# A hybrid decoder layer on one core: output tiles ahead of the last head's decays, a pin on a second group of side work, and token operands made inside the delta rule

## The chip, the cores and the metric

The kernel runs on one core of a Trainium2 chip. The metric is the device time of one execution in microseconds (us); lower is better. The engines are named as in the profile: PE (TensorE), DVE (VectorE), ACT (ScalarE), POOL (GpSimd) and SP (SyncE, which here only issues transfers). Each engine executes its own instructions strictly in the order in which they stand in its queue.

## What is computed

One layer over 1024 tokens of width 1024, in float32: a SwiGLU feed-forward block of width 2816 (FFN1), a mixer, a second feed-forward block (FFN2), a final norm.

```
x += 0.5 * swiglu(rms_norm(x))                       # FFN1
proj = rms_norm(x) @ w_in                            # q,k,v,z of 8 delta-rule heads; x,z,B,C of the SSM
o_gdn = gated_delta_rule(conv_silu(q), conv_silu(k), conv_silu(v), g, beta)   # 8 heads of 128
o_gdn = rms_norm(o_gdn) * silu(z)
o_ssm = grouped_rms_norm((ssd_scan(xs, dt, a, B, C) + xs * d) * silu(z_ssm))  # 16 heads of 64
x += concat(o_gdn, o_ssm) @ w_out
x += 0.5 * swiglu(rms_norm(x))                       # FFN2
out = rms_norm(x)
```

In the delta rule a head's keys are normalised to unit length, and a chunk's triangular system is solved from the decayed products of the keys with themselves.

## The kernel before

A float32 product is made of three matmuls of rounded parts: each operand is split into `hi` (a cast on ACT) and `lo` (a subtraction on DVE), and `mm3` (L123 to L125) adds hi*hi, lo*hi and hi*lo in one PSUM bank. Sums of quadrants (a seven-product scheme) save matmuls in the feed-forward blocks and in half of the projections; their sums are further DVE work. PSUM has four groups of banks by tag: `pj` with three banks, `mx` with two, `sc` with two, `oo` with one. A list scheduler lays out each engine's queue from the order of the program, the pools' buffers, and pins: inside `with tc.issue_after(ins)` an instruction stands behind `ins` on that one's engine.

FFN1 (`gate_up_all`) runs over steps `i`, in each of which `prep(grp)` makes the next weights' operands for two groups (`as` sums on DVE at L317, `ah` casts on ACT at L241, `al` differences on DVE). It also draws on a generator `side` of weight units for the mixer (`win_units`): a unit is loaded (`wraw`), summed (`wsum`), split (`wunit`) and stored in DRAM (`wu_scr`). In FFN2 the generator is empty. A silu at L380 is the first function of FFN1 on ACT that needs another table (ACT_TABLE_LOAD).

The mixer goes through the SSM in four units `un` of the loop that follows, then through the delta rule's eight heads `h`. The heads 0 to 3 (`NESTED` = 4) are projected by `mm3` through `proj_half`; the heads 4 to 7 by `chunk`, which multiplies the stored weight units (`wunits`) with token operands: sums of token quadrants, made by `token_operands(k)` (11 sums on DVE, four casts `thi`, four subtractions `tlo`, eight stores to `t_scr`) and loaded again by `first_token_tiles`, `token_tile` and others.

A head runs so: `dt` holds its decays (a load, an exponential `qe` at L1361, a causal mask on POOL, eight exponentials at L1364); q, k and v are convolved and put through silu; `k_part` transposes the keys (L1345, eight matmuls into two `mx` banks) and reads each of the eight blocks twice on ACT, `jd` (L1349, a square with its sum) and `kd` (L1350, a scaled copy); the products of the keys (L1426, L1427) use the same two `mx` banks; then come the triangular solve (`fs_u`, `fx`, `ft`, `fs_x`, `lv`), which goes through DRAM, and a chain of eight state steps (L1534 to L1556, with `vn` and `vr` on ACT). The state steps of head h - 1 are interleaved with the projections of head h. `qsq` (L1448) reuses the buffer of `zc`, and so stands behind the store of it to `z_scr`.

In the last head the first output tiles fill PE: `out_start` loads the first SSM group `y` and rows `x` of w_out, splits `x` into `w` and `y` into `mtt` (ACT at L1200, DVE at L1201), and `group_tile(0, b, dh)` for four values of `b` and two of `dh` makes eight tiles of six matmuls in `pj`; ACT scales each into `xa` (L1220), which empties its bank. `group_prep(1)` makes the operands of the next SSM group (`whi`, `wlo` of the weights, `mtt` from `nat`). The remaining groups follow, and then the tiles of the delta rule's heads.

Of the kernel before, what the change touches and what calls it, by code (L numbers as in the profile page):

```python
# [11 lines left out]
F32 = mybir.dt.float32  # L12
F32R = mybir.dt.float32r
# [31 lines left out]
def kernel(  # L45
# [182 lines left out]
    def hsl(h, k, s):  # L228
        return h[k // 2][:, k % 2, s]
# [124 lines left out]
    def gate_up_all(pool, H, w_gate, w_up, scr, raws, ops, last, work, tail, side):  # L354
# [66 lines left out]
        for i, (p, w) in enumerate(todo):  # L421
# [7 lines left out]
            def prep(grp):  # L429

                if nxt:
                    made = a_ops(pool, *((raws[0], m, nxt[0]) for m in A_GROUPS[grp]))
                    if i == 2 and grp == 0:
                        first_hid(made)
                    with ExitStack() as pins:
                        if i == 4 and grp == 0:
                            for e in made:
                                pins.enter_context(tc.issue_after(e.ins))
                        for _ in range(0 if i < 4 else 2 if grp and i % 3 == 1 else 1):
                            next(side, None)  # L440
                elif tail:
                    tail.pop(0)()
                if raws and grp == 1:
                    next_load()
# [541 lines left out]
    def token_operands(k):  # L986

        b11, b12, b21, b22 = ([hsl(t, k + 4 * i, slice(j * 512, (j + 1) * 512)).bitcast(F32) for t in (hhi, hlo)]
                              for i in range(2) for j in range(2))

        def put(m, t):
            hi = tt.tile([P, 512], F32R, name="thi")
            lo = tt.tile([P, 512], F32R, name="tlo")
            split(hi, lo, t)
            for i, part in enumerate((hi, lo)):
                nc.sync.dma_start(out=t_scr[m][:, i, k], in_=part.bitcast(F32))

        def step(t, x, y, op):
            V.tensor_tensor(out=t, in0=x, in1=y, op=op)

        t = tt.tile([P, 512], F32, name="tsum")
        step(t, b22[0], b12[0], ALU.subtract)
        step(t, t, b22[1], ALU.add)
        step(t, t, b12[1], ALU.subtract)
        put(7, t)
        step(t, t, b11[0], ALU.add)
        step(t, t, b11[1], ALU.add)
        put(6, t)
        step(t, b22[0], t, ALU.subtract)
        step(t, t, b22[1], ALU.add)  # L1010
        put(5, t)
        for x, y in ((b21[0], b22[0]), (b21[1], b22[1])):
            step(t, t, y, ALU.subtract)
            step(t, t, x, ALU.add)
        put(4, t)

    tt = cs_.enter_context(tc.tile_pool(name="tokens", bufs=1, side="right", reuse_waits="tile"))
    rstd_g = []
    for un in range(4):
# [36 lines left out]
        token_operands(un)  # L1056
# [154 lines left out]
    def group_tile(n, b, dh, w, m):  # L1211
        bs = slice(b * P, (b + 1) * P)
        ds = slice(dh * 512, (dh + 1) * 512)
        p = psum("pj")
        for j in range(2):
            last = mm3(p, m[0][:, j, bs], m[1][:, j, bs], w[0][:, j, ds], w[1][:, j, ds], j == 0, j == 1)
        o = out_bufs[0][b // 2][:, b % 2, ds]
        r = rstd_g[n // 2][:, b:b + 1]
        if n == 0:
            A.mul(out=o, in_=p, mul=r)  # L1220
        else:
            V.scalar_tensor_tensor(out=o, in0=p, scalar=r, in1=o, op0=ALU.mult, op1=ALU.add)
        return last

    FIRST_TILES = 4
    out_bufs, ready0 = [], []

    def out_start():
# [8 lines left out]
        for j in range(2):  # L1237
            split(w[0][:, j], w[1][:, j], x[:, j])
            ssm_split(0, j, y, *m)
# [87 lines left out]

    slots, H_IN = [], {}
# [3 lines left out]
    first_token_tiles()  # L1332
    with ExitStack() as cg:
        g1 = cg.enter_context(tc.tile_pool(name="gdn1", bufs=1, reuse_waits="tile"))
        g2 = cg.enter_context(tc.tile_pool(name="gdn2", bufs=2, reuse_waits="tile"))
        def k_part(h, kt):
# [4 lines left out]
            for half in range(2):  # L1341
# [4 lines left out]
                for i in range(4):  # L1346
# [3 lines left out]
                    A.mul(out=kd[:, b], in_=pt[:, i * P:(i + 1) * P], mul=wend[:, b, h:h + 1])  # L1350
# [5 lines left out]
        for h in range(GH):  # L1356
            hl = h % 2
# [5 lines left out]
            for b in range(NB):  # L1363
                A.activation(out=dt[:, b], in_=dt[:, b], func=AF.Exp, bias=ngc[:, b, h:h + 1])  # L1364
            qt = gp.tile([P, L], F32, name="qt", tag="xst", bufs=2)
            kt = g2.tile([P, L], F32, name="kt", bufs=3)
            vt_ = g1.tile([P, L], F32, name="vt_")
            if h < NESTED:
# [3 lines left out]
                tk, br2, kd = k_part(h, kt)  # L1372
                wa = next_w()
                if h == NESTED - 1:
                    first_units()
                    token_tile(6)
# [11 lines left out]
            else:  # L1388
# [11 lines left out]
                tk, br2, kd = k_part(h, kt)  # L1400
                with tc.issue_after(copy.ins):
                    A.activation(out=qt, in_=qt, func=AF.Silu)
                if h == GH - 1:
                    out_start()
                conv_from(pre, 16 + h, vt_)
                A.activation(out=zc, in_=zc, func=AF.Silu)
                A.activation(out=vt_, in_=vt_, func=AF.Silu)
            nc.sync.dma_start(out=z_scr[h], in_=zc)
            if h == GH - 1:
                ready1 = group_prep(1)  # L1410
                for b in range(FIRST_TILES):
                    for dh in range(2):
                        tile_end = group_tile(0, b, dh, *ready0[0])
# [6 lines left out]
            for b0 in range(0, NB, 2):  # L1420
# [8 lines left out]
                for i in range(2):  # L1429
# [5 lines left out]
                                in1=dt[:, b2], op=ALU.mult)  # L1435
            fs_u = dram.tile([4, NB, 32, 32], F32, name="fs_u", bufs=2)
# [121 lines left out]

            sso = g2.tile([P, NB], F32, name="sso")
# [178 lines left out]
```

## Time and profile before

| | |
|---|---|
| median of 3 runs | 2318.16 us (2317.92 to 2319.36) |
| profiled execution, its own time | 2318.03 us |
| span in the profile | 2316.3 us |
| mean granted clock of PE | 0.993 |
| busy: PE, DVE, ACT, POOL | 2267.1, 1753.3, 1179.7, 50.6 us |

The profile is of one execution. A row of a timeline has the start and the duration of an instruction or of several in a row, the engine, the line, the operation, out<-in, and in brackets how long the engine stood idle ahead of it and what ended that. A row of the waits has the engine and line that waited, the engine and line that ended the wait, and the total, the number and the longest. A row of a stretch has the busy time (and number of instructions) of PE, of its weight loads, of DVE, ACT and POOL, then the clock granted to PE, where 1.00 is full, and two figures on transfers.

### The profile page before, as it was taken

How to read it: one execution, taken by the hardware profiler on the slowest of the kernel's cores; microseconds unless marked ns; L12 is line 12 of the kernel's file. 1: busy time of each engine (PE TensorE's matmuls, PEld its weight loads, DVE VectorE, ACT ScalarE, POOL GpSimd, SP SyncE). 2: the span in 40 equal slices, each digit the busy share in tenths (PEclk: the TensorE clock that was granted, in tenths of full speed). 3: DMA queues.
4: the chain of work that ended last, by engine and by line, in shares of the span. 5: the costliest groups of instructions: out<-in, count | busy, mean ns of one | idle time of the engine just before them, and what ended most of it. 6: DMA issues, size and time to landing. Idle time of an engine off the chain costs nothing.

```text
span 2316.3 us, 31987 instructions
## 1 busy us (share of the span) xinstructions
PE 2267.1 (98%) x11654; PEld 1848.9 (80%) x11654; DVE 1753.3 (76%) x3217; ACT 1179.7 (51%) x2284; POOL 50.6 (2%) x117
## 2 busy tenths in 40 slices
PE   7999999999999999999999998999999999999998
PEld 5788888888878878877877776888878888888886
DVE  8998987769777787656667778578698777766787
ACT  7444433354367985874655557432443333334344
POOL 0000000000000110000000000000000000000000
PEclk9999999999999999999999999899999999999999
DMA  3467663496653343242356556335223333329445
GB/s 111 159 210 241 228 207 115 170 334 214 210 187 125 128 128 98 69 128 65 83 165 180 168 172 216 103 98 191 91 72 119 109 106 109 104 89 357 138 154 214
DMA packets 262194, 356.96 MB, mean 154 GB/s; under 512 B 60808, under 2 KB 167404, under 8 KB 260244
## 3 DMA queue, kind: packets, MB, share of 16 engines
q1 hardware_dynamic: 261364, 352.73, 46.7%
q8 instruction: 91, 1.49, 0.3%
q0 software_dynamic: 672, 2.19, 0.2%
q14 instruction: 67, 0.55, 0.1%
HBM read 249.34 MB, written 105.52 MB: 153 GB/s over the span
## 4 chain that ended last, share of the span: by engine, by line
PE 79%; DVE 9%; ACT 7%; DMA 2%; issue 2%; POOL 0%; SPq 0%; DVEq 0%; ACTq 0%; POOLq 0%
PE ps_pj L124 6%; PE ps_pj L123 6%; PE ps_pj L125 6%; PE ps_pj L334 6%; PE ps_pj L335 6%; PE ps_pj L336 6%; PE ps_mx L334 3%; PE ps_mx L336 3%; PE ps_mx L335 3%; PE ps_pj L564 2%; PE ps_pj L565 2%; PE ps_pj L563 2%; PE ps_pj L1259 2%; PE ps_pj L1261 2%; PE ps_pj L1260 2%
## 5 line engine op out<-in xcount | busy, mean ns | idle before, releaser
L336 PE MATMUL ps_pj<-bh,al 128*128 128x512 f32 x688 | 267.9, 389 | 0.0
L335 PE MATMUL ps_pj<-bl,ah 128*128 128x512 f32 x688 | 267.8, 389 | 0.0
L334 PE MATMUL ps_pj<-bh,ah 128*128 128x512 f32 x688 | 267.5, 390 | 0.0
L125 PE MATMUL ps_pj<-hhi,wlo 128*128 128x512 f32 x576 | 229.9, 399 | 0.0
L123 PE MATMUL ps_pj<-hhi,whi 128*128 128x512 f32 x576 | 229.4, 398 | 0.4 <-ACT gsb L901 0.4
L124 PE MATMUL ps_pj<-hlo,whi 128*128 128x512 f32 x576 | 228.9, 397 | 0.0
L335 PEld LDWEIGHTS ps_pj<-bl,ah 128*128 128x128 f32 x688 | 129.2, 188 | 26.7
L336 PEld LDWEIGHTS ps_pj<-bh,al 128*128 128x128 f32 x688 | 129.2, 188 | 26.7
L334 PEld LDWEIGHTS ps_pj<-bh,ah 128*128 128x128 f32 x688 | 129.0, 188 | 26.6
L242 DVE TENSOR_TENSOR al<-as,ah 128x512 fp32r<-128x512 f32 x220 | 141.1, 685 | 7.3 <-ACT ah L241 6.8
L317 DVE TENSOR_TENSOR as<-wst 128x512 f32<-128x512 f32 x220 | 144.3, 684 | 2.5 <-DMA wst<-in_ffn_w_up_dram 2.4
L241 ACT CAST ah<-wst 128x512 fp32r<-128x512 f32 x88 | 54.5, 621 | 179.1 <-PE ps_oo L335 116.7
L241 ACT CAST hid<-hraw 128x1024 fp32r<-128x1024 f32 (+1 forms) x84 | 82.2, 980 | 123.6 <-PE ps_oo L565 45.6
L334 PE MATMUL ps_mx<-bh,ah 128*128 128x512 f32 x352 | 139.3, 398 | 5.2 <-ACT sg L380 2.1
L335 PE MATMUL ps_mx<-bl,ah 128*128 128x512 f32 x352 | 139.0, 395 | 0.4 <-DVE bl L242 0.4
L336 PE MATMUL ps_mx<-bh,al 128*128 128x512 f32 x352 | 138.2, 393 | 1.0 <-DVE al L242 1.0
L241 ACT CAST ah<-as 128x512 fp32r<-128x512 f32 x220 | 125.2, 617 | 19.6 <-DVE as L317 19.5
L123 PEld LDWEIGHTS ps_pj<-hhi,whi 128*128 128x128 f32 x576 | 108.4, 188 | 21.6 <-ACT gsb L901 0.9
L124 PEld LDWEIGHTS ps_pj<-hlo,whi 128*128 128x128 f32 x576 | 108.4, 188 | 21.4 <-issue 0.8
L125 PEld LDWEIGHTS ps_pj<-hhi,wlo 128*128 128x128 f32 x576 | 108.3, 188 | 20.9 <-issue 0.5
L242 DVE TENSOR_TENSOR hid<-hraw,hid 128x1024 fp32r<-128x1024 f32 (+1 forms) x84 | 95.0, 1131 | 26.6 <-ACT hid L241 26.3
L343 ACT COPY m<-ps_pj 128x512 f32<-128x512 f32 x88 | 51.6, 588 | 112.9 <-PE ps_pj L336 112.7
(502 smaller groups left out, 5651.6 us busy)
## 6 DMA issues: line engine op xcount, KB each, us to landing
hraw<-hid_scr SPq DMA_DIRECT2D x70, 512.0 KB, 4.3
wu_scr<-wunit SPq DMA_DIRECT2D x112, 256.0 KB, 3.2
wunits<-wu_scr SPq DMA_DIRECT2D x56, 512.0 KB, 4.7
hid_scr<-hs SPq DMA_DIRECT2D x110, 256.0 KB, 3.0
wst<-in_ffn_w_down_dram SPq DMA_DIRECT2D x50, 512.0 KB, 4.7
wst<-in_ffn_w_gate_dram SPq DMA_DIRECT2D x22, 1024.0 KB, 5.6
wst<-in_ffn_w_up_dram SPq DMA_DIRECT2D x22, 1024.0 KB, 5.5
hid_scr<-sg SPq DMA_DIRECT2D x44, 256.0 KB, 2.0
```

What stands on the lines that cost most here:

```text
L123: T.matmul(o, lhsT=wh, rhs=mh, start=first, stop=False)
L124: T.matmul(o, lhsT=wh, rhs=ml, start=False, stop=False)
L125: return T.matmul(o, lhsT=wl, rhs=mh, start=False, stop=last)
L241: return (A.copy(out=hi, in_=src), V.tensor_tensor(out=lo, in0=src, in1=hi.bitcast(F32), op=ALU.subtract))
L242: V.tensor_tensor(out=lo, in0=src, in1=hi.bitcast(F32), op=ALU.subtract))
L317: V.tensor_tensor(out=t, in0=v[0], in1=v[1], op=v[2])
L334: T.matmul(bank, lhsT=wh[:, k], rhs=bh[:, k], start=a, stop=False, skip_group_check=True)
L335: T.matmul(bank, lhsT=wh[:, k], rhs=bl[:, k], start=False, stop=False, skip_group_check=True)
L336: T.matmul(bank, lhsT=wl[:, k], rhs=bh[:, k], start=False, stop=z, skip_group_check=True)
L343: A.copy(out=t, in_=bank)
L563: T.matmul(bank, lhsT=hh, rhs=wh, start=first and k == 0, stop=False, skip_group_check=True)
L564: T.matmul(bank, lhsT=hh, rhs=wl, start=False, stop=False, skip_group_check=True)
```

## The change

Four edits. The pin in `gate_up_all` holds the side work of both groups at step 4. `token_operands` goes from the four SSM units to the ends of heads 0 (two calls), 1 and 2 of the delta rule, in buffers of another pool with two pairs of halves; `first_token_tiles` follows to head 3. `k_part` of the heads 0 to 3 goes behind the projections of v and z. In the last head `out_start` and the eight output tiles come first, then `k_part` (its `kd` on DVE), the decays, and v and z; `out_start` makes both halves of `mtt` ahead of `w`; the store of z is issued by POOL; and `group_prep(1)` stands behind the key products, pinned behind the sixth `xa`.

```diff
@@ gate_up_all
-                        if i == 4 and grp == 0:
+                        if i == 4:
                             for e in made:
                                 pins.enter_context(tc.issue_after(e.ins))
@@ SSM units
         proj_z(zts)
-        token_operands(un)
...
@@ out_start
         for j in range(2):
+            ssm_split(0, j, y, *m)
+        for j in range(2):
             split(w[0][:, j], w[1][:, j], x[:, j])
-            ssm_split(0, j, y, *m)
...
@@ group_tile
-            A.mul(out=o, in_=p, mul=r)
+            moved.append(A.mul(out=o, in_=p, mul=r))
...
@@ token_operands, put
+        halves = natp.tile([P, 4, 512], F32R, name="halves", tag="zg")
...
+            parts = [halves[:, m % 2 * 2 + i] for i in range(2)]
+            split(*parts, t)
...
@@ k_part
-                    A.mul(out=kd[:, b], in_=pt[:, i * P:(i + 1) * P], mul=wend[:, b, h:h + 1])
+                    if h == GH - 1:
+                        V.tensor_scalar(out=kd[:, b], in0=pt[:, i * P:(i + 1) * P],
+                                        scalar1=wend[:, b, h:h + 1], scalar2=None, op0=ALU.mult)
+                    else:
+                        A.mul(out=kd[:, b], in_=pt[:, i * P:(i + 1) * P], mul=wend[:, b, h:h + 1])
@@ heads (decays(h) is the block of qe and dt, now a function)
+            if h < GH - 1:
+                qe, dt = decays(h)
...
                 conv_silu(g1, wa, 1, cw_g, 8 + h, kt)
-                tk, br2, kd = k_part(h, kt)
                 wa = next_w()
                 if h == NESTED - 1:
+                    first_token_tiles()
                     first_units()
...
-                tk, br2, kd = k_part(h, kt)
+                if h < GH - 1:
+                    tk, br2, kd = k_part(h, kt)
...
-                if h == GH - 1:
+                if h < GH - 1:
+                    conv_from(pre, 16 + h, vt_)
+                    A.activation(out=zc, in_=zc, func=AF.Silu)
+                    A.activation(out=vt_, in_=vt_, func=AF.Silu)
+                else:
                     out_start()
-                conv_from(pre, 16 + h, vt_)
-                A.activation(out=zc, in_=zc, func=AF.Silu)
-                A.activation(out=vt_, in_=vt_, func=AF.Silu)
-            nc.sync.dma_start(out=z_scr[h], in_=zc)
-            if h == GH - 1:
-                ready1 = group_prep(1)
-                for b in range(FIRST_TILES):
-                    for dh in range(2):
-                        tile_end = group_tile(0, b, dh, *ready0[0])
+                    for b in range(FIRST_TILES):
+                        for dh in range(2):
+                            tile_end = group_tile(0, b, dh, *ready0[0])
+                    tk, br2, kd = k_part(h, kt)
+                    qe, dt = decays(h)
+                    conv_from(pre, 16 + h, vt_)
+                    A.activation(out=zc, in_=zc, func=AF.Silu)
+                    A.activation(out=vt_, in_=vt_, func=AF.Silu)
+            (G if h == GH - 1 else nc.sync).dma_start(out=z_scr[h], in_=zc)
+            if h < NESTED:
+                tk, br2, kd = k_part(h, kt)
...
+            if h == GH - 1:
+                with tc.issue_after(moved[5].ins):
+                    ready1 = group_prep(1)
...
+            for k in ((0, 1), (2,), (3,))[h] if h < 3 else ():
+                token_operands(k)
```

What this does to the queues is seen at three places. The first is ACT's queue at the start of FFN1, around the silu at L380; before:

```order
L241 CAST bh_651<-bs 128x512 x2
L241 CAST ah<-wst 128x512
L241 CAST wunit<-wraw 128x512
L241 CAST ah<-as 128x512
L380 ACT_TABLE_LOAD
L380 ACTIVATE sg_759<-ps_pj 128x512
L380 ACTIVATE sg_760<-ps_mx 128x512
L241 CAST ah<-as 128x512 x2
L241 CAST ah<-wst 128x512
```

and now:

```order
L241 CAST bh_651<-bs 128x512 x2
L241 CAST ah<-wst 128x512
L241 CAST ah<-as 128x512
L380 ACT_TABLE_LOAD
L380 ACTIVATE sg_759<-ps_pj 128x512
L380 ACTIVATE sg_760<-ps_mx 128x512
L241 CAST ah<-as 128x512 x2
L241 CAST ah<-wst 128x512
```

The casts of the side units (`wunit<-wraw`) no longer stand around the silu.

The second is ACT's queue in the last head, from the first operand half `mtt` of the output tiles on (`vr` belongs to head 6, `xa` empties an output bank). Before, its eight `jd` and `kd` follow the last row here, and the second `mtt` stands behind them:

```order
L1200 ACTIVATE mtt<-y_13586,cols 128x1024
L1567 ACTIVATE vr<-vr,co 128x128 x8
L1361 ACT_TABLE_LOAD
L1361 ACTIVATE qe<-dt 128x1024
L241 CAST w_13589<-x_13585 128x1024 x2
L1364 ACTIVATE dt<-dt,ngc 128x128 x8
L1349 ACTIVATE jd,tk<-ps_mx 128x128
```

and now:

```order
L1167 ACTIVATE mtt<-y_13499,cols 128x1024
L1588 ACTIVATE vr<-vr,co 128x128 x8
L1167 ACTIVATE mtt<-y_13499,cols 128x1024
L241 CAST w_13502<-x_13498 128x1024 x2
L1364 ACT_TABLE_LOAD
L1364 ACTIVATE qe<-dt 128x1024
L1260 ACTIVATE vt__13280<-pre,cols 128x1024
L1187 ACTIVATE xa<-ps_pj,rg_7083 128x512
L1367 ACTIVATE dt<-dt,ngc 128x128 x3
L1187 ACTIVATE xa<-ps_pj,rg_7083 128x512
L1367 ACTIVATE dt<-dt,ngc 128x128 x3
L1187 ACTIVATE xa<-ps_pj,rg_7083 128x512
```

Both `mtt` and both casts of `w` are ahead of the exponentials, and the `xa` stand among these. Further on, where the `jd` now are (`whi` and `mtt<-nat` are of `group_prep(1)`):

```order
L1187 ACTIVATE xa<-ps_pj,rg_7083 128x512
L1348 ACTIVATE jd,tk<-ps_mx 128x128
L138 CAST whi<-wst 128x1024
L1348 ACTIVATE jd,tk<-ps_mx 128x128
L138 CAST whi<-wst 128x1024
L1167 ACTIVATE mtt<-nat,cols 128x1024
L1348 ACTIVATE jd,tk<-ps_mx 128x128
L1167 ACTIVATE mtt<-nat,cols 128x1024
L1348 ACTIVATE jd,tk<-ps_mx 128x128
```

The `kd` are gone from ACT, and the casts of the next group stand between the `jd`.

The third is PE's queue at the end of the last projection; before:

```order
L1260 MATMUL ps_pj<-t_10853,wunits 128x512
L1261 MATMUL ps_pj<-t_10851,wunits 128x512
L1345 MATMUL ps_mx<-ident,kt 128x128 x8
L123 MATMUL ps_pj<-w_13589,mtt 128x512
L124 MATMUL ps_pj<-w_13590,mtt 128x512
L125 MATMUL ps_pj<-w_13589,mtt 128x512
```

and now, 48 matmuls of output tiles after the same last product:

```order
L124 MATMUL ps_pj<-w_13503,mtt 128x512
L125 MATMUL ps_pj<-w_13502,mtt 128x512
L1344 MATMUL ps_mx<-ident,kt 128x128 x8
L123 MATMUL ps_pj<-w_13502,mtt 128x512
L124 MATMUL ps_pj<-w_13503,mtt 128x512
```

The transposes went from ahead of the first output tile to behind the eighth of them, and 18 more matmuls behind the transposes come the key products:

```order
L124 MATMUL ps_pj<-w_13503,mtt 128x512
L125 MATMUL ps_pj<-w_13502,mtt 128x512
L1442 MATMUL ps_mx<-kt 128x128
L1443 MATMUL ps_mx<-qt,kt 128x128
L1442 MATMUL ps_mx<-kt 128x128
```

Before, these stood among the state steps, more than 100 rows behind the transposes.

More of the change, by code (lines that the diff above doesn't have):

```diff
@@ L984, in token_sums @@
         nc.sync.dma_start(out=dst, in_=scr.rearrange("j (c p) -> p (j c)", p=P))
[L986 to L1017, printed above, removed]
     rstd_g = []
@@ L1225 @@
     FIRST_TILES = 4
-    out_bufs, ready0 = [], []
+    out_bufs, ready0, moved = [], [], []
     def out_start():
@@ L1326, in other_token_tiles, with token_operands, put, step @@
         token_tile(4)
+    def token_operands(k):
+        b11, b12, b21, b22 = ([hsl(t, k + 4 * i, slice(j * 512, (j + 1) * 512)).bitcast(F32) for t in (hhi, hlo)]
+                              for i in range(2) for j in range(2))
+        halves = natp.tile([P, 4, 512], F32R, name="halves", tag="zg")
+        def put(m, t):
+            parts = [halves[:, m % 2 * 2 + i] for i in range(2)]
+            split(*parts, t)
+            for i, part in enumerate(parts):
+                nc.sync.dma_start(out=t_scr[m][:, i, k], in_=part.bitcast(F32))
+        def step(t, x, y, op):
+            V.tensor_tensor(out=t, in0=x, in1=y, op=op)
+        t = natp.tile([P, 4, 512], F32, name="tsum", tag="nat")[:, 0]
+        step(t, b22[0], b12[0], ALU.subtract)
+        step(t, t, b22[1], ALU.add)
+        step(t, t, b12[1], ALU.subtract)
+        put(7, t)
+        step(t, t, b11[0], ALU.add)
+        step(t, t, b11[1], ALU.add)
+        put(6, t)
+        step(t, b22[0], t, ALU.subtract)
+        step(t, t, b22[1], ALU.add)
+        put(5, t)
+        for x, y in ((b21[0], b22[0]), (b21[1], b22[1])):
+            step(t, t, y, ALU.subtract)
+            step(t, t, x, ALU.add)
+        put(4, t)
     slots, H_IN = [], {}
@@ L1331 @@
     natp = cn.enter_context(tc.tile_pool(name="natp", bufs=1, side="right", reuse_waits="tile"))
-    first_token_tiles()
     with ExitStack() as cg:
@@ L1354, in k_part, with decays @@
             return tk, br2, kd
-        for h in range(GH):
-            hl = h % 2
+        def decays(h):
             qe = g2.tile([P, L], F32, name="qe")
@@ L1364 @@
                 A.activation(out=dt[:, b], in_=dt[:, b], func=AF.Exp, bias=ngc[:, b, h:h + 1])
+            return qe, dt
+        for h in range(GH):
+            hl = h % 2
+            if h < GH - 1:
+                qe, dt = decays(h)
             qt = gp.tile([P, L], F32, name="qt", tag="xst", bufs=2)
```

## The prediction

> **What bounds the kernel now.** I read the page first, then the engines' busy time by stretches of 50 us, then the list of waits, and only then single instructions at the places that these point to. TensorE (PE) carries the kernel:
>
> ```profile
> PE 2267.1 (98%) x11654; PEld 1848.9 (80%) x11654; DVE 1753.3 (76%) x3217; ACT 1179.7 (51%) x2284; POOL 50.6 (2%) x117
> ```
>
> So a change that adds no matmul can gain at most the 2316.3 - 2267.1 = 49.2 us in which PE stands still, and what PE loses by running at a lower clock. Where these lie is seen from stretches (columns: busy time and instructions of each engine, then the granted clock):
>
> ```profile
> 1010.00:1180.00 170.00, 169.23 (x1066) 136.19 (x1064) 115.09 (x354) 106.56 (x262) 8.35 (x30) 1.00 0.30 78
> 1400.00:1450.00 50.00, 41.07 (x256) 31.24 (x255) 43.37 (x121) 37.77 (x88) 2.70 (x4) 0.89 0.67 219
> 1450.00:1500.00 50.00, 49.74 (x275) 40.33 (x275) 26.39 (x84) 25.41 (x68) 0.73 (x5) 0.90 0.33 98
> ```
>
> The first row is the delta rule's early heads: PE is full there, and VectorE (DVE) and ScalarE (ACT) have a third of their time free. The other two are the last head and what follows it: 9 us idle, and a clock of 0.9 over 100 us. The list of waits names the idle time (total, times, longest, in us):
>
> ```profile
> PE ps_pj L123 <- ACT xa L1220: 4.9, 2, 4.7
> ...
> PE ps_pj L123 <- ACT mtt L1200: 2.9, 1, 2.9
> PE ps_mx L1426 <- ACT kd L1350: 2.5, 3, 1.4
> PE ps_mx L334 <- ACT sg L380: 2.1, 1, 2.1
> PE ps_mx L1345 <- ACT kt L862: 1.8, 2, 1.6
> ```
>
> All five wait for ACT, and none for a transfer. I take them in the order of time, as three places.
>
> **Place A, FFN1 near 72 us: the pin.** PE waits 2.1 us for the silu at L380. What came ahead of that silu:
>
> ```profile
> 68.94 0.68 DVE L317 TENSOR_TENSOR as<-wst 128x512 f32<-128x512 f32 x1
> ...
> 70.45 0.62 ACT L241 CAST wunit<-wraw 128x512 fp32r<-128x512 f32 x1 [3.44 <-DMA wraw<-in_w_in_dram]
> 70.98 0.62 ACT L241 CAST ah<-as 128x512 fp32r<-128x512 f32 x1
> 71.61 1.28 ACT L380 ACT_TABLE_LOAD   x1
> 72.91 0.60 ACT L380 ACTIVATE sg<-ps_pj 128x512 f32<-128x512 f32 x1
> 73.40 0.59 ACT L380 ACTIVATE sg<-ps_mx 128x512 f32<-128x512 f32 x1
> ```
>
> ACT executes in order. It stood 3.44 us at the first cast of a side unit, whose operand was still in flight, and the cast of `ah` behind it had its input from DVE at 68.94 + 0.68 = 69.62. The change takes the unit's cast away from here. Then `ah` starts at about 69.65, its 0.62 leads to the table load at 70.27, 1.28 later the two silus, the second of them ending at 72.65 instead of 73.99. PE resumes 1.35 us earlier, and its wait shrinks from 2.1 to about 0.8. What PE did after the wait:
>
> ```profile
> 74.05 0.79 PE L334 MATMUL ps_mx<-bh,ah 128*128 128x512 f32 x1 [2.13 <-ACT sg L380]
> 74.64 0.63 PE L335 MATMUL ps_mx<-bl,ah 128*128 128x512 f32 x1
> 75.06 0.63 PE L336 MATMUL ps_mx<-bh,al 128*128 128x512 f32 x1
> ...
> 77.56 0.40 PE L336 MATMUL ps_mx<-bh,al 128*128 128x512 f32 x1
> 77.79 0.40 PE L334 MATMUL ps_mx<-bh,ah 128*128 128x512 f32 x1
> ```
>
> Matmuls start 0.42 us apart and later 0.23: PE ran at half clock until about 77.4, for 3.4 us, which cost half of them, 1.7 us. With a wait of 0.8 I expect no drop. Place A: -1.35 - 1.7 = -3.05. Ends: -1.35 if the drop comes all the same, and -3.8, if the rest of the wait goes too. The Trainium skill, "TensorE: Matmul & The Clock Gate", Part 1 with its section on HAM oscillation, says that the clock halves after an idle window of about 3.4 us, and gives as the rule to have no idle gaps above that. The trace differs: a 2.13 us gap was followed by half clock. By the rule as written the gap would have cost no clock, place A would be worth 1.35 alone, and the sum would be 1.7 us less.
>
> Not removed but moved are the side units (casts on ACT, subtractions on DVE, loads and stores on SP). They come a step or two later and closer together; behind one that waits for its store stand PSUM copies. I cost this at nothing, since PE is covered by three pj banks, with ends of 0 and +3.4, the idle time of the cast above, should one such wait come to lie open. Unit order in FFN2 doesn't change, as it has no side work.
>
> **Place B, the Mamba units and heads 0 to 3: token operands and `k_part`.** What moves (durations in ns, min/median/max):
>
> ```profile
> L999 DVE TENSOR_TENSOR tsum<-tsum,hlo x24: 679/691/694, 721.9 to 890.1; 128x512 f32<-128x512 f32 x24
> L241 ACT CAST thi<-tsum x16: 602/617/657, 725.0 to 890.9; 128x512 fp32r<-128x512 f32 x16
> ```
>
> Each of the four calls has 11 steps and 4 subtractions on DVE, 15 x 0.69 = 10.4 us, 4 casts on ACT, 2.5 us, and 8 stores on SP. Three calls' worth ends in heads 0 to 2 (two of them in head 0). In 170 us there DVE has 170 - 115 = 55 us and ACT 63 us free, and 4 x 10.4 = 41.6 and 9.9 are added: they fit, at 92% of DVE. I take 0. Ends: below, -1.6, should the Mamba units gain as much as the largest single wait of that size (head 3's, next paragraph) from being rid of them; above, +7.5, if in each of three heads one cast holds ACT as long as its like in the page's longest wait of this kind, 2.5 us (kd). Covered is all this by PE's projection matmuls between the state steps; without that cover the 41.6 us would lie on the path.
>
> `k_part` of heads 0 to 3 (eight transposes on PE, then `jd` and `kd` on ACT) goes behind the v and z projections. PE gets 24 matmuls of 0.23 us ahead of the transposes and as many ahead of the products that need `kd`. Head 0's kd waits, 2.5 us in the list, should go except for a rest of 0.2: -2.3. The transposes' wait for `kt`, 1.6 us (L1345), may go by the same 5.5 us of shift; in heads 1 and 2, however, the order now puts the products close behind the transposes, where a wait of 1.4 (the longest of kd) is possible in each. I let these two cancel. Place B: -2.3, ends -5.5 and +7.5.
>
> **Place C, the last head, 1415 to 1460 us.** ACT's queue there:
>
> ```profile
> 1426.98 2.44 ACT L1364 ACTIVATE dt<-dt,ngc 128x128 f32<-128x128 f32 x8
> ...
> 1433.32 1.23 ACT L1200 ACTIVATE mtt<-y,cols 128x1024 fp32r<-128x1024 f32 x1
> ...
> 1437.87 1.98 ACT L138 CAST whi<-wst 128x1024 fp32r<-128x1024 f32 x2
> 1440.06 1.06 ACT L1407 ACTIVATE vt__13327<-vt__13327 128x1024 f32<-128x1024 f32 x1 [0.21 <-DVE vt__13327 L847]
> 1441.02 2.17 ACT L1200 ACTIVATE mtt<-nat,cols 128x1024 fp32r<-128x1024 f32 x2
> 1443.10 1.82 ACT L1220 ACTIVATE xa<-ps_pj,rg 128x512 f32<-128x512 f32 x3
> ```
>
> PE has its first output tiles from about 1428. It waits 2.9 us for the second `mtt`, which stands behind the eight exponentials and the eight `jd`/`kd`; then three tiles fill the three pj banks, and PE waits 4.7 us until ACT comes to the first `xa`, which empties one. The clock that follows:
>
> ```profile
> 1435.00:1440.00 5.00, 3.49 (x9) 1.95 (x7) 5.00 (x7) 4.82 (x5) 0.00 (x0) 0.66 0.31 48
> 1440.00:1445.00 5.00, 1.18 (x2) 0.50 (x2) 5.00 (x7) 4.86 (x6) 0.00 (x0) 0.78 0.66 195
> 1445.00:1450.00 5.00, 4.94 (x88) 3.38 (x88) 1.52 (x6) 2.73 (x5) 0.00 (x0) 0.50 0.84 343
> 1450.00:1455.00 5.00, 5.00 (x26) 3.84 (x26) 1.23 (x1) 2.93 (x6) 0.00 (x0) 0.50 0.00 0
> 1455.00:1460.00 5.00, 5.00 (x24) 4.17 (x23) 1.81 (x2) 1.56 (x2) 0.00 (x0) 0.51 0.15 16
> ```
>
> The loss by clock is the busy time times the missing part of the clock: 3.49 x 0.34 = 1.2, then half of 1.18 + 4.94 + 5 + 5, 8.0. With 2.9 + 4.7 = 7.6 us of waits, place C loses 16.8 us.
>
> After the change ACT has both `mtt` and both casts of `w` ahead of the exponentials, and these alternate with the `xa` (0.31 us for an exponential, 0.61 for an `xa`). Output tiles take PE 6 x 0.23 = 1.4 us each, and between two `xa` lie at most three exponentials, or a table load and one activation, 1.28 + 1.06 = 2.3 us: three banks cover that. So PE can run its 48 matmuls from 1428 to 1439 without a wait; the two waits go, and with them the half clock. What is late next: the transposes now end at about 1440.2, 18 matmuls follow (to 1444.3), and then the products wait until four `jd` on ACT and four `kd` on DVE have read the first bank. Between these `jd` ACT now has two `whi` and two `mtt` casts, 1.98 + 2.17 = 4.15, and four pairs of `jd` and `kd` that wait for each other take some 0.4 each: 1440.2 + 5.8 = 1446.0. A new wait of about 1.8 us, with `xa` and the rest of the tiles queued behind the `jd`. Its ends: 0 (all of the pairs fall between the casts) and 3.5, and a clock drop of 1.7 may follow, as after the gap of 2.1 at place A.
>
> The store of z leaves SP for POOL's queue, where a memset stands ahead of it that waits for the solve's short DVE chain; `qsq` on ACT waits until it has landed, and four `jd` wait behind that:
>
> ```profile
> 1431.76 0.30 POOL L1507 MEMSET lv<- 32x256 f32 x1 [5.36 <-DVE ft L1476]
> DMA to landing us min/median/max: 6.0/7.3/8.7
> ```
>
> The second row is that of the eight z stores. The solve's chain now shares DVE with three operand halves of 1.2 to 1.3 us that came behind it, so the memset moves to about 1436, and the store lands by 1436.3 + 8.7 = 1445, before `qsq`'s turn at 1446. Cost 0, ends 0 and 2. DVE's eight `kd` are off ACT, and DVE had 5.00 of 5 busy only until 1445. Place C: -16.8 + 1.8 = -15.0, ends -17 and -9.
>
> **The sum.** -3.05 - 2.3 - 15.0 = -20.35 us against the profiled execution's 2318.03 (span 2316.3, and 1.7 around it), which lies 0.13 below the median of 2318.16. That gives 2297.7 and, put on the median, 2297.8; I say 2298.
>
> **The rivals.** (1) The wait at C changes its place: the `jd`/`kd` pairs, `qsq` and the z store take the 3.5 us end and 2 more, with two drops of 1.7 of the clock. Then C gives -16.8 + 8.9 = -8, and the time is 2318 - 3 - 2.3 - 8 = 2305. For it: ACT and DVE are both full in 1435 to 1445 above, and the work there doesn't shrink. Against: the first 48 matmuls need none of it. (2) Slower: the token operands stall heads 0 to 2. Each cast waits on ACT for the store that read its half, and the state steps' `vn` stand behind it. It would have to cost more than 20.4 + 4.6 = 25 us, or 1.6 us for each of the 16 casts with nothing of it covered; by the 1.4 that the worst kd wait cost it would be 22, and the time 2320. Against: PE was busy 169.2 of 170 us there although the state chain waits at every step. (3) The change doesn't reach C's second wait: if PE fills three banks before ACT reaches the first `xa` as now, 4.7 us and the 8.0 of clock stay, and the time is 2310.5. Against: the order has four `xa` ahead of the z silu. (4) More is gained: the Mamba units' waits, `kt`, and no new wait at C: 2298 - 1.6 - 1.6 - 1.8 = 2293. (5) A's half clock was not set off by its gap, and stays: of three gaps of PE named in the list above 2 us, the one at A is the shortest, and only one drop beside the last head's stands against it. Then A gives 1.35 alone, and the time is 2299.5. The rule of the Trainium skill quoted at place A ("TensorE: Matmul & The Clock Gate", HAM oscillation) would lead to this, and says nothing else of this change.
>
> **How the numbers follow.** The forecast, 2294 to 2302: 0.50. (5), which lies within that: 0.05. Rival (1), 2302 to 2309: 0.19. (4): 0.11. (3): 0.07. (2) in a mild form, 10 to 20 us lost, 2308 to 2318: 0.05; in full, above 2322.8: 0.03. 0.2%, 4.6 us, is about what a measurement of this kernel can tell from no change. Slower by more than that: 0.03; within it: 0.04, from half of (2)'s mild form and the top of (3); faster: 0.93. The range is 2291 to 2309: below lies the edge of (4), above (2), (3) and the edge of (1).
>
> **What would show it.** After the change: no half clock in 70 to 80 us, and a wait at L380 under 1 us; no PE wait on `kd` above 0.5 us in head 0; in 1428 to 1440 PE busy throughout at full clock, with 48 output matmuls ahead of the eight transposes; one new wait of 1 to 3 us of the products behind them. Wrong I am if a clock drop stays in the last head, if the casts of the halves show in the waits of heads 0 to 2, or if the bunched side units open a wait in 100 to 150 us.

## The result, and the profile after

The changed kernel takes 2305.47 us (median of 6 runs, 2302.14 to 2311.24) against 2318.04 before (6 runs beside it): 12.6 us less, a ratio of 0.995 with a 95% interval of 0.9936 to 0.9964. The profiled execution is the fastest of its six, with 2302.14 us, a span of 2300.4 and so 15.9 us less than the profiled one before. The runs differ by the granted clock: 0.998 in the profiled one, 0.995 in the slowest. 0.003 of 2300 us are some 7 of the 9.1 us between these two.

The stretches shown of before, here of the changed kernel (with one more, 1180 to 1400, in which PE was busy for 218.59 of 220 us before):

```profile
1010.00:1180.00 170.00, 168.27 (x1057) 134.73 (x1056) 135.19 (x401) 100.52 (x259) 6.11 (x28) 1.00 0.49 146
1180.00:1400.00 220.00, 212.27 (x1514) 168.96 (x1512) 147.58 (x464) 128.06 (x370) 11.01 (x28) 0.99 0.58 167
1400.00:1450.00 50.00, 48.47 (x265) 38.94 (x264) 41.87 (x113) 39.49 (x84) 3.75 (x5) 1.00 0.62 202
1450.00:1500.00 50.00, 49.98 (x344) 40.06 (x339) 40.06 (x128) 25.86 (x69) 0.73 (x5) 1.00 0.38 125
```

The last head has its clock back (1.00 instead of 0.89 and 0.90) and 7.6 us more of PE's busy time. The heads 3 to 6 have lost what they had: PE stands still for 7.7 us in 1180 to 1400, where it was full before. The list of waits says the same (its rows for transfers at the start left out):

```profile
PE ps_mx L1442 <- ACT kd L1353: 4.3, 5, 1.1
...
PE ps_mx L1442 <- DVE kd L1350: 1.4, 1, 1.4
...
PE ps_sc L1541 <- ACT u L1531: 0.9, 1, 0.9
...
PE ps_mx L334 <- ACT sg L380: 0.8, 1, 0.8
```

The waits for `xa`, `mtt` and `kt` are gone. The wait for `sg` has shrunk from 2.1 to 0.8, and the one for `kd` has grown from 2.5 us in 3 places to 4.3 in 5.

**Place A** came as forecast. ACT's queue, and PE behind it:

```profile
69.77 0.62 ACT L241 CAST ah<-as 128x512 fp32r<-128x512 f32 x1 [2.64 <-DVE as L317]
70.41 1.28 ACT L380 ACT_TABLE_LOAD   x1
71.70 0.60 ACT L380 ACTIVATE sg<-ps_pj 128x512 f32<-128x512 f32 x1
72.19 0.59 ACT L380 ACTIVATE sg<-ps_mx 128x512 f32<-128x512 f32 x1
...
72.84 0.50 PE L334 MATMUL ps_mx<-bh,ah 128*128 128x512 f32 x1 [0.80 <-ACT sg L380]
73.17 0.39 PE L335 MATMUL ps_mx<-bl,ah 128*128 128x512 f32 x1
```

PE resumes at 72.84 instead of 74.05, and the next matmuls are 0.24 us apart, at full clock. At the end of FFN1's first part the kernel is 3.5 us ahead.

**Place C** too: from 1428 to 1440 PE works without a wait, and behind the 18 matmuls that follow the transposes stands the new wait, of 1.4 us (the first two rows). ACT and DVE ahead of its end (the rows from 1440.69 on) show what it is made of: between the four `jd` stand two `whi` and two `mtt` casts, the four `kd` wait in DVE's queue behind the second halves of the same operands, and the last of them ends at 1446.36.

```profile
1439.80 1.04 PE L1344 MATMUL ps_mx<-ident,kt 128*128 128x128 f32 x8
1446.42 0.49 PE L1442 MATMUL ps_mx<-kt 128*128 128x128 f32 x2 [1.37 <-DVE kd L1350]
...
1440.69 0.28 ACT L1348 ACTIVATE jd<-ps_mx 128x128 bf16<-128x128 f32 x1
...
1444.38 1.17 ACT L1167 ACTIVATE mtt<-nat,cols 128x1024 fp32r<-128x1024 f32 x1
1445.42 0.29 ACT L1348 ACTIVATE jd<-ps_mx 128x128 bf16<-128x128 f32 x1
...
1444.83 1.27 DVE L1168 SCALAR_TENSOR_TENSOR mtt<-nat,cols,mtt 128x1024 fp32r<-128x1024 f32 x1
1446.02 0.34 DVE L1350 TENSOR_SCALAR kd<-ps_mx,wend 128x128 f32<-128x128 f32 x1
...
1430.00:1435.00 5.00, 5.00 (x23) 4.04 (x22) 5.00 (x9) 4.80 (x12) 0.39 (x1) 1.00 0.50 185
1435.00:1440.00 5.00, 5.00 (x24) 3.98 (x23) 1.07 (x5) 4.97 (x7) 0.86 (x2) 1.00 0.33 104
```

**What was lost** stands in the stretch of head 4. First PE's waits near 1266 us in the changed kernel, then the stretch around them, before and after:

```profile
1265.66 0.24 PE L1522 MATMUL ps_sc<-lv 32*32 32x32 f32 x2 [0.61 <-DVE lv L1518]
...
1267.38 1.11 PE L1536 MATMUL ps_sc<-lv,u 64*64 64x64 f32 x16 [0.56 <-ACT lv L1529]
1269.43 1.56 PE L1541 MATMUL ps_sc<-u,lv 64*64 64x64 f32 x16 [0.94 <-ACT u L1531]
```

```profile
1240.00:1300.00 60.00, 59.88 (x417) 47.83 (x416) 43.42 (x127) 31.41 (x87) 2.13 (x7) 1.00 0.59 162
1240.00:1300.00 60.00, 56.03 (x393) 44.91 (x392) 40.63 (x130) 26.76 (x81) 1.04 (x6) 0.97 0.49 145
```

The rows are the second to fourth of the four steps of head 3's triangular solve; each waits until ACT or DVE has moved a result of the steps ahead of it out of PSUM. 3.41 us of half clock follow. In PE's queue no output or projection matmul stands between them now. Before there were ten. To compare kernels I take the time between two marks on PE less its matmuls at their usual pace, and call it the loss; a part of it is common to all kernels. In us, half clock included:

| kernel | Mamba units | heads, to key products of 4 | of 4 to 5 | rest of heads | last head and tiles |
|---|---|---|---|---|---|
| before | 19.2 | 21.9 | 4.7 | 10.5 | 30.4 |
| after | 16.7 | 20.7 | 11.9 | 12.3 | 13.7 |

The Mamba units are the SSM units; "to key products of 4" ends where head 4's begin. The last head gained 16.7 us, the Mamba units 2.5, the early heads 1.2; the stretch between the key products of heads 4 and 5 lost 7.2, the rest of the heads 1.8.

### The profile page after: what moved, and what is told of

The parts are those of the page before. It is cut to its first block, busy times and chain, and to the rows that moved or that the text cites. A ratio compares the mean times of both kernels' runs of the same rounds, so it can differ in the third digit from the quotient of the medians.

```text
span 2300.4 us, 31969 instructions
## 1 busy us (share of the span) xinstructions
PE 2256.9 (98%) x11654; PEld 1842.6 (80%) x11654; DVE 1743.3 (76%) x3225; ACT 1171.8 (51%) x2272; POOL 53.2 (2%) x118
## 5 line engine op out<-in xcount | busy, mean ns | idle before, releaser
L336 PE MATMUL ps_pj<-bh,al 128*128 128x512 f32 x688 | 268.1, 390 | 0.0
L336 PEld LDWEIGHTS ps_pj<-bh,al 128*128 128x128 f32 x688 | 129.2, 188 | 26.5
L336 PE MATMUL ps_mx<-bh,al 128*128 128x512 f32 x352 | 137.7, 391 | 0.3 <-DVE al L242 0.3
L124 PEld LDWEIGHTS ps_pj<-hlo,whi 128*128 128x128 f32 x576 | 108.5, 188 | 20.7 <-issue 0.8
```

Of the source, the lines that this page charges most:

```text
L124: T.matmul(o, lhsT=wh, rhs=ml, start=False, stop=False)
L336: T.matmul(bank, lhsT=wl[:, k], rhs=bh[:, k], start=False, stop=z, skip_group_check=True)
```

## The experiments

Four theories of this loss were tested. Theory K: late `k_part` sets the key products too close behind the transposes. Theory T: the token operands' work on DVE and ACT delays the heads. Theory S: the order is to blame, with no matmuls left between the solve's steps. Later, theory D: the operands' sums delay the solves through DVE's queue. Times are medians of 4 to 17 runs. `before` beside them had 2317.1 to 2318.5.

**The pin alone.**

```diff
-                        if i == 4 and grp == 0:
+                        if i == 4:
```

> The kernel before with the pin on both groups of side work and nothing else. All theories agree on place A: PE's wait for the silu at L380 falls from 2.1 to 0.8 us, no half clock at 74 to 77 us, 3 us saved (2 to 4); everything behind 200 us as before, only earlier. If the moved side units cost something, a new PE wait shows in 100 to 450 us and the gain is under 2 us.

2315.28 against 2317.14 us, 1.9 less, ratio 0.9991 (0.9982 to 1.0). The stretches of place A:

```profile
70.00:75.00 5.00, 4.17 (x19) 3.13 (x18) 3.73 (x7) 3.61 (x7) 0.00 (x0) 1.00 0.14 34
75.00:80.00 5.00, 5.00 (x24) 4.10 (x23) 4.92 (x9) 3.21 (x6) 0.00 (x0) 1.00 0.12 20
```

The half clock is gone, and in the profile the marks from FFN1's end to head 6 come 3.4 to 3.9 us earlier; no new wait opened, so the side units cost nothing that shows. The medians give about half of that, with an interval that reaches to no change; how the half clock falls elsewhere differs from run to run (last section).

**The two moves, apart.** Three kernels: late `k_part` undone; the token operands back in the Mamba units (with the buffers that they had there, and `first_token_tiles` back ahead of the heads); both.

```diff
                 conv_silu(g1, wa, 1, cw_g, 8 + h, kt)
+                tk, br2, kd = k_part(h, kt)
...
-            if h < NESTED:
-                tk, br2, kd = k_part(h, kt)
```

> The changed kernel with k_part of heads 0 to 3 back ahead of the v and z projections; token operands stay in heads 0 to 2. Theory S (the loss in heads 3 to 6 comes from the order: with both edits together no output matmuls are left between the steps of head 3's solve): the solve of head 3 has 12 matmuls between its steps again, and the kernel gains 18 us or more against before (2300 or less). Theory K (late k_part alone puts the key products too close behind the transposes): the same gain, 18 us. Theory T (the token operands' work on DVE and ACT delays the heads): the gain stays at 12 to 13 us.

```diff
         proj_z(zts)
+        token_operands(un)
...
-            for k in ((0, 1), (2,), (3,))[h] if h < 3 else ():
-                token_operands(k)
```

> The changed kernel with the token operands back in the Mamba units; late k_part stays. Theory S: 10 matmuls lie between the steps of head 3's solve, and the gain is 18 us or more against before, less 1 to 3 us for head 0, whose solve has only 2 now. Theory K: the gain stays at 12 to 13 us, with waits of the key products for kd of 0.7 to 1.3 us in heads 1 to 6. Theory T: 18 us or more.

Both diffs together:

> The kernel before with the pin and the last head's edits alone (k_part and the token operands where they were). All theories: A's 3 us and the last head's 16.6 us are gained whole, 19 to 20 us against before, about 2298.5; head 0's two waits for kd (1.4 and 0.9 us) are there again. If the gain is near 12 us, the loss in heads 3 to 6 comes from neither move and the three theories fall.

| kernel | us | ratio (95%) | loss, heads 4 to 5 |
|---|---|---|---|
| `k_part` back, tokens in heads | 2306.15 | 0.9954 (0.9942 to 0.9967) | 7.1 |
| tokens back, `k_part` late | 2298.29 | 0.992 (0.9906 to 0.9933) | 5.7 |
| both back | 2298.67 | 0.9922 (0.991 to 0.9935) | 4.7 |

With both back the pin and the last head's edits are left alone: 18.5 us faster than `before` beside them (2317.14), about 2298.5 as expected. Theory K falls: late `k_part` in four heads costs and gains nothing that can be told. Its waits for `kd` in five heads belong to the tokens' move as well; with the tokens back PE waits for `kd` twice, 0.8 us in all, and for `xa` in the last head instead:

```profile
PE ps_pj L123 <- ACT xa L1220: 2.2, 2, 2.0
...
PE ps_mx L1443 <- ACT kd L1355: 0.8, 2, 0.4
```

The tokens' move costs 7 us, with either place of `k_part`. With both back PE has the stretch of head 4 full again:

```profile
1240.00:1300.00 60.00, 59.99 (x419) 48.13 (x417) 43.13 (x133) 31.68 (x97) 2.19 (x7) 1.00 0.59 162
```

Theory S expected 2300 or less with `k_part` back, where the order has 12 matmuls between the steps; it got 2306. In its profile 6.8 of the 7.7 us against the kernel with both back are half clock, behind waits in head 0 and the last head, and its five runs lie within 1.3 us: the loss there is another than in the changed kernel.

**Other orders with the same operands.** Late `k_part` in head 0 alone, with the tokens in the Mamba units and in the heads, and then three token calls in head 0 and one in head 1:

```diff
+                if h >= 1:
+                    tk, br2, kd = k_part(h, kt)
...
-            if h < NESTED:
+            if h < 1:
```

> Pin, last head, late k_part in head 0 alone; token operands in the Mamba units. Every solve up to head 5's has 10 or more output matmuls between its steps in PE's order. Theory S (the order decides: what matters is how many matmuls lie between the solve's steps): head 0's waits for kd (2.7 us and 1.7 of clock in the run with both moves undone) go and nothing else changes, 2295 to 2297, 1 to 3 us under the run with late k_part in four heads. Theory K (late k_part itself brings waits for kd): the same, as three of four heads have it early. If it is 2298 or more, head 0's waits were hidden already.

> The changed kernel, but k_part late in head 0 alone; token operands stay in heads 0 to 2. In PE's order head 3's solve has 12 matmuls between its steps (none in the changed kernel). Theory S: the 6 us of head 3's solve and its clock drop go, the Mamba units keep their 2.4 us, 2296 to 2299. Theory T (the operands' work itself on DVE and ACT delays the heads, wherever the order puts the matmuls): 2303 to 2307, with the loss between the key products of heads 4 and 5 still above 7 us (4.7 before).

```diff
-            for k in ((0, 1), (2,), (3,))[h] if h < 3 else ():
+            for k in ((0, 1, 2), (3,), ())[h] if h < 3 else ():
```

> The changed kernel with three of the four token calls in head 0 and the fourth in head 1, so that none is in head 2; k_part late in four heads. Same work on DVE and ACT in the heads as the changed kernel; in PE's order head 3's solve has 8 matmuls between its steps and head 4's 4. Theory S: the stretch of head 4 loses 5 to 7 us instead of 11.9, 2299 to 2302. Theory T: head 0 has half more of it and gets slower, the sum stays at 2304 to 2308.

The first took 2301.25 (0.9931, 0.9919 to 0.9943), not the 2295 to 2297 expected: head 0's waits went, but head 2 now has two of 1.0 and 0.9 us for `kd`, and head 5 one of 1.6. The second took 2299.96 (0.9927, 0.9915 to 0.9939), with a loss of 6.6 us in the stretch of head 4: the operands' place is the changed kernel's, and 5.3 us are back; it lies 1 us above theory S's range and 3 below theory T's. With the operands in the heads, then, late `k_part` gains 6.2 us in head 0 (2306.15 to 2299.96), and being late in heads 1 to 3 too takes 5.5 back (2305.47), which the comparison of none with four had hidden. The third took 2320.02, no better than before (1.0003, 0.9993 to 1.0013), and missed both theories. Its waits:

```profile
PE ps_mx L1442 <- ACT kd L1353: 4.2, 2, 3.7
PE ps_sc L1515 <- DVE lv L1509: 3.7, 1, 3.7
```

It lost 20.8 us in the stretch of head 4, with 13.7 us at half clock there. So the same 60 DVE instructions of operands cost nothing that can be told (2299.96 against 2301.25, with `k_part` late in head 0 alone) or some 20 us (2320.02, with three calls in head 0, against 2298.29, both late in four heads), depending on the order.

**The matmuls put back by pins.** In the changed kernel three weight units of head 5's projection are held behind steps of head 3's solve:

```diff
-        unit_prod(y, 7, False)
+        with tied(0):          # behind the last matmul of the solve's first step
+            unit_prod(y, 7, False)
...                             # unit 3 behind the second step, unit 4 behind the third
```

> The changed kernel with three pins more and nothing else: three weight units' products (12 matmuls each) in head 5's first projection are held behind the first three steps of head 3's solve, so that PE's order has 12 matmuls between these steps instead of none. Token operands, k_part and the last head as changed. Theory S: the stretch of head 4 loses 5 to 7 us instead of 11.9, without half clock, and the time is 2298 to 2301. Theory T (the operands' work on DVE and ACT): the loss only moves to the pinned products, 2304 to 2307.

2303.45 (0.9937, 0.9923 to 0.995): 2 us under the changed kernel, with intervals that overlap. The solve's later steps wait no more, but the first one does, for 1.1 us. Half clock left out, the stretch loses 9 us, against 10.2 in the changed kernel; the profiled execution, the slowest of the five, has 13.65 us of half clock there besides. The order between the steps is not the whole cause.

**Fewer sums.** The kernel leaves out 10 of the 11 sums, and not 8 as the expectation says, so 6.9 us for each call; its output is not the layer's.

```diff
-            V.tensor_tensor(out=t, in0=x, in1=y, op=op)
+            if y is b12[0]:
+                V.tensor_tensor(out=t, in0=x, in1=y, op=op)
```

> The changed kernel without 8 of the 11 sums of each token_operands call (the casts, subtractions and stores stay, of unfinished sums): 8 x 0.69 = 5.5 us less on DVE for each call in heads 0 to 2. Theory D (the operands' sums in DVE's queue stretch the triangular solves of heads 2 and 3, 80 us from the key products to the solve's last step in head 3 against 71 before, and PE then waits for them): head 3's solve comes back to 70 to 75 us, the stretch of head 4 loses 5 to 6 us instead of 11.9, 2297 to 2301. Theory S (only the number of matmuls between the solve's steps in PE's order counts, and three pins that put 12 there gained 2 us): 2302 to 2304, with the solve still 80 us long.

2300.58 (0.9922, 0.9909 to 0.9934), 4.9 us under the changed kernel and inside theory D's range; the stretch of head 4 loses 4.8 us, as before the change. (With the sums gone the scheduler also set another order, with 13 matmuls between the steps of head 3's solve; so this run doesn't part the sums from the order. Twelve matmuls put there by pins had made 2 us.)

```profile
1240.00:1300.00 60.00, 60.00 (x414) 47.93 (x413) 41.47 (x130) 29.02 (x88) 2.13 (x7) 0.98 0.55 152
```

The way from the sums to head 4 can be followed in part. The sums run at 983 to 1106 us, and DVE is busy for 66.7 us of the 72 from 1008 to 1080 (46.4 in the kernel with both moves undone). Head 1's key products start at 1058 us in the changed kernel and at 1059 in the kernel with both moves undone. The last step of its solve, in these two and in the one without the sums (where the products start at 1061):

```profile
1144.98 1.14 PE L1541 MATMUL ps_sc<-u,lv 64*64 64x64 f32 x16
...
1130.82 1.14 PE L1541 MATMUL ps_sc<-u,lv 64*64 64x64 f32 x16
...
1132.68 1.14 PE L1542 MATMUL ps_sc<-u,lv 64*64 64x64 f32 x16
```

With the sums head 1's solve is 12 to 14 us later. PE hardly waits for it then, it has projections to do. Head 2's solve isn't late: from key products to its end it takes 68 us, against 72 before. Late `k_part` moves the projections ahead besides: the first weight unit starts at 1183.8 us, against 1202.0 before (1182.6 with late `k_part` and the tokens back). So head 4's projection is early, head 3's solve is not, and the solve meets the v convolution on DVE too. Its DVE chain (`ft`, `fx`), 62 instructions, took 26.4 us before and 32.1 after; the rows are the whole chains, before and after:

```profile
1218.66:1245.10 26.44, 26.32 (x121) 20.90 (x120) 24.29 (x88) 16.14 (x34) 1.13 (x2) 1.00 0.70 209
...
1218.34:1250.40 32.06, 31.96 (x158) 25.94 (x156) 30.58 (x101) 23.40 (x61) 2.03 (x2) 1.00 0.63 194
```

DVE is the full engine in both, with 6.3 us more of other work in the second, 3.8 of them the v convolution. Without the sums the chain takes 26.0 us again. That convolution stands in head 3's chain in the three kernels that have all sums in heads 0 to 2 as the changed one and differ in `k_part` alone (chains of 30.4 to 32.1 us), and in none of those without them there (`before`, both back, tokens back, fewer sums: up to 28.3). From key products to the solve's end head 3 takes 80.4 us in the changed kernel, 70.7 before, and 76.4 without the sums, so theory D's 70 to 75 was missed by a little. Theory D gives the delay, and the order where PE pays for it. For this speaks that head 3 takes 83 us with late `k_part` in head 0 alone too, but with 12 matmuls between the steps of its solve the stretch of head 4 loses 6.6 us there, not 11.9. That both are needed is how I read these runs together. How sums that end at 1106 us push the v convolution into a chain at 1218, with head 2's solve on time between them, isn't shown, and why the scheduler chose each order is left open.

**The sums on POOL,** with `k_part` in its old place:

```diff
-            V.tensor_tensor(out=t, in0=x, in1=y, op=op)
+            G.tensor_tensor(out=t, in0=x, in1=y, op=op)
```

> The changed kernel with k_part of heads 0 to 3 in its old place and the token operands' 11 sums on POOL instead of DVE (nothing left out). Theory D: DVE is as free in heads 0 to 2 as with the operands in the Mamba units, less 4 subtractions; the solve of head 3 takes 70 to 75 us (83.6 in the kernel with k_part back and the sums on DVE), the Mamba units keep their 2.4 us, 2296 to 2299, the best of all. Rival: POOL's sums slow DVE beside them, or come too late for their stores, and it is 2302 or more.

2329.9 (1.0051, 1.0037 to 1.0064), slower than before: the rival's case, and far from 2296 to 2299. PE's waits, the sums on POOL, and what stands behind them in POOL's queue:

```profile
PE ps_mx L1344 <- ACT kt L862: 11.8, 3, 9.6
PE ps_mx L1441 <- DVE dt L1448: 8.5, 2, 8.2
...
L1310 POOL TENSOR_TENSOR tsum<-tsum,hlo x24: 1258/1306/2296, 976.2 to 1103.7; 128x512 f32<-128x512 f32 x24
...
1041.89 0.11 POOL L853 MEMSET pre<- 128x3 f32 x1
```

A sum takes 1.3 us there, up to 2.3, instead of 0.69, and a memset of 0.1 us that head 1's k convolution needs stands behind them. Nearly all of the loss is in heads 0 and 1; PE is full in head 4, and head 3's solve takes 70.7 us.

**The last head.** `kd` back on ACT:

> The changed kernel with the last head's kd on ACT as before, all else as changed. If DVE's kd is what keeps ACT free for the casts and xa, ACT gets 8 x 0.25 = 2 us more and PE's wait ahead of the last head's key products grows from 1.5 to 2.5 us or more, with half clock behind it in most runs: 2307 to 2310. If instead the pairs of jd and kd that wait for each other across two engines are what makes the wait, it shrinks to under 1 us and the time is 2303 to 2305.

2304.54 (0.9943, 0.993 to 0.9956), not to be told from the changed kernel. PE's wait ahead of the first key product is gone, but one of 0.75 us opens between the key products, for DVE, and one of 0.8 at head 6's solve:

```profile
1450.20 0.46 PE L1442 MATMUL ps_mx<-kt 128*128 128x128 f32 x2 [0.75 <-DVE dt L1449]
1452.11 0.21 PE L1515 MATMUL ps_sc<-lv,u 32*32 32x32 f32 x1 [0.78 <-DVE lv L1509]
```

On ACT the eight `jd` and `kd` now follow each other with no cast between them, so this run doesn't part the change of engine from the change of order.

With the three pins of above, and the casts and `qsq` behind the fourth `jd`:

```diff
-                with tc.issue_after(moved[5].ins):
+                with tc.issue_after(squares[-5].ins):     # squares: the jd
...
-            A.activation(out=qsq, in_=qt, func=AF.Square)
+            with tc.issue_after(squares[-5].ins) if h == GH - 1 else nullcontext():
+                A.activation(out=qsq, in_=qt, func=AF.Square)
```

> As the kernel with the three pins, and in the last head the casts of the next group (whi, mtt) and qsq on ACT are pinned behind the fourth jd. By the prediction's step, the casts between the jd make PE's new wait ahead of the last head's key products (1.4 to 1.5 us): it then shrinks under 0.3 us, and 1 to 3 us are saved (more than the wait where half clock followed it), 2296 to 2299. Rival: the tiles' xa, now behind the casts, hold PE's pj banks instead, and a wait of 1 us or more stands there: no gain.

2308.21 (0.9961, 0.9948 to 0.9973), 4.8 us more than with the pins alone. The wait for `kd` is gone, but no time was saved, and the rival came (the first of the rows is head 6's solve, the second a tile that waits for `xa`):

```profile
1447.84 0.21 PE L1525 MATMUL ps_sc<-lv,u 32*32 32x32 f32 x1 [1.76 <-DVE lv L1519]
1449.51 0.79 PE L123 MATMUL ps_pj<-w,mtt 128*128 128x512 f32 x1 [0.98 <-ACT xa L1187]
```

10.2 us of half clock followed. The order of the changed kernel is the better one here.

## Why the prediction was right or wrong

2298 was forecast, in 2291 to 2309, faster with 0.93; it came to 2305.47, in the range and faster, with 12.6 of the 20.35 us of the sum. It lies outside the 2294 to 2302 that had half of the chance, and at the very time of rival (1); that is luck, as rival (1) had the loss in the last head, and it came elsewhere. The places A and C together were right: the kernel with the pin and the last head's edits alone gains 18.5 us for the 18.05 forecast. Place B, which that kernel leaves out, cost 6.8 us instead of gaining 2.3.

- **Place A, -3.05.** Right: the wait is 0.80 as worked out, no half clock follows, and 3.5 us are gained at FFN1's first part. The wait at L336 some 25 us later shrank from 1.0 to 0.3 as well. The moved side units cost nothing that shows. By medians the pin alone makes 1.9 us, and the 95% interval reaches from nothing to 4. Rival (5) falls, since the half clock went with the gap: none of the 13 profiles with the pin has it in 70 to 80 us. The Trainium skill ("TensorE: Matmul & The Clock Gate", HAM oscillation) gives the rule to have no idle gaps above about 3.4 us. In this place the trace differs from it: 3.41 us of half clock followed a gap of 2.13 us; after one of 0.80 there was none.
- **Place C, -15.0.** Right: -16.7 by the losses. The two waits and their half clock went, 48 matmuls run through, the new wait stands where it was put and measures 1.4 for the forecast 1.8. Rivals (1) and (3) fall in the profile. The casts between the `jd` and the pairs across two engines are seen in the trace, as the step had them. Which of the two makes the wait isn't shown, since both experiments take the casts away, and nothing is won by removing it: with `kd` on ACT two waits of 0.8 open, with the casts moved away larger ones.
- **Place B, `k_part`, -2.3.** Head 0's two waits for `kd` went, as did the one for `kt`. But waits of 0.5 to 1.1 for `kd` opened in five heads, 4.3 us in all. They come only with the tokens in the heads: with the tokens in the Mamba units late `k_part` leaves 0.8 us of them, none in heads 1 and 2, and still makes only 0.4 us by medians. What it gained ahead of head 4 it lost behind: 1 us in the stretch of head 4, and in the last head a wait of 2.0 for `xa` with half clock behind it. The forecast priced the move at its own place, and it changed the order of what follows.
- **Place B, token operands, 0.** This is the step that failed, as a term that was mis-sized. Against the kernel with the tokens back, the move costs 7.2 us. The Mamba units' gain, which I took as 0 with an end of -1.6, is 2.4 to 2.6 us; the heads pay 8.4 by the losses in the profile, more than the end of +7.5. "They fit, at 92% of DVE" took the mean of 170 us, and all four calls, not three, lie in heads 0 to 2: the sums crowd into a part of the stretch, in which DVE is 93% busy (66.7 of 72 us), against 80% in the whole (135.19 of 170). PE is as full there as I said (168.27 of 170), but the solves of heads 0 and 1, behind the sums in DVE's queue, end 13 and 14 us later than with both moves undone, and PE pays 100 us later, in head 3's solve, where my cover, the projections, has been used up. For the sums as the reason speaks the kernel that leaves them out (4.9 us), though its order changed too; the way from them to head 3's solve is in part my reading, and what the moved buffers and `first_token_tiles` do of it was not tried alone. In another order, with late `k_part` in head 0 alone, the same operands in the same place cost nothing that can be told. Rival (2) named the operands but the wrong place and queue: no cast on ACT waiting for a store carried it, and the loss stayed under the 10 to 20 us of its mild form.
- The rest, 3.3 us between the profiled execution and the median, goes with the granted clock, 0.998 in the profiled one and 0.995 to 0.997 in the other five.

The kernel with the pin and the last head's edits alone, and the one with late `k_part` as well, are the fastest that ran: 2298.67 and 2298.29 us, 6.8 and 7.2 under the changed kernel. The one with the operands in the heads and late `k_part` in head 0 alone, 2299.96, can't be told from them.

## What to carry to other kernels

A stretch with free time on an engine can take work with hardly a wait there, and still lose: what counts is whether a chain runs through that engine's queue, and whether the engine that covers it has work left when the chain comes in late. Follow the chain a round or two of the loop further than the edit, and take an engine's free time where the work will land, not as a mean over the stretch. Where a scheduler sets the order, an edit that is free in one order can cost 20 us in the next: undo each edit with the others in place. Moving a step early where PE has no work of its own, as with the output tiles here, pays twice, as idle time and as clock.

## What the hardware showed that I had not expected

The same gap need not have the same price. At the start of FFN2 every kernel has a wait of 1.4 us for `bh`. In the kernel with the three pins half clock of 3.41 us followed it, in the changed kernel none (5 us stretches from the same phase of the program; the first two rows are the kernel with the pins):

```profile
1690.00:1695.00 5.00, 3.07 (x8) 2.12 (x8) 4.86 (x9) 2.16 (x5) 0.00 (x0) 0.78 1.03 342
1695.00:1700.00 5.00, 5.00 (x21) 4.05 (x20) 4.88 (x9) 1.39 (x3) 0.00 (x0) 0.88 0.19 62
...
1685.00:1690.00 5.00, 3.07 (x13) 2.18 (x13) 4.87 (x8) 2.17 (x5) 0.00 (x0) 1.00 1.06 349
1690.00:1695.00 5.00, 5.00 (x24) 4.04 (x23) 4.88 (x9) 1.92 (x4) 0.00 (x0) 1.00 0.18 57
```

It followed in 4 of the 14 profiles. All half-clock stretches but the one at each execution's end are 3.41 us or multiples of it long, and after a gap of 1.4 to 2 us there came none, one or three. So in this kernel a gap of this length has a chance of 1.7 us or more on top of itself, and a profile shows one draw: compare medians, and count what a removed gap is worth with its chance, not with the draw of one trace.
